# The order of the three products of a split matmul: the low activation before the low weight

## The chip, the core and the metric

The kernel runs on one core of one Trainium2 chip. The metric is the device time of one execution in microseconds (us), as the median of several runs. Beside the timed runs there is one profiled execution, with a trace of every instruction of each engine. In the rows PE is the matmul engine, PEld its weight load, DVE the vector engine, ACT the scalar engine, POOL the GpSimd engine and SP the queue that issues most transfers.

## The reference

One layer of a streaming encoder, 256 frames of 2048 channels in float32. A gated feed-forward block, a mixer with two branches, and a second feed-forward block follow each other, each added to the residual stream.

```python
h = rms_norm(x, ffn1_norm[l])
x = x + 0.5 * swiglu(h, ffn1_w_gate[l], ffn1_w_up[l], ffn1_w_down[l])      # 2048 -> 2 x 5504 -> 2048
h = rms_norm(x, mix_norm[l])
proj = h @ w_in[l]                                                          # 2048 -> 11280 columns
(gq, gk, gv, gz, ga, gb, aq, ak, av, gate_gdn, gate_att) = jnp.split(proj, split_at, axis=-1)
o_gdn = gdn_branch(...)                                                     # gated DeltaNet, 8 heads
o_att = chunk_attention_branch(...)                                         # banded softmax, 8 heads
merged = (jax.nn.sigmoid(gate_gdn) * (o_gdn @ w_branch_gdn[l])
          + jax.nn.sigmoid(gate_att) * (o_att @ w_branch_att[l]))
x = x + merged @ w_out[l]
h = rms_norm(x, ffn2_norm[l])
x = x + 0.5 * swiglu(h, ffn2_w_gate[l], ffn2_w_up[l], ffn2_w_down[l])
```

Nearly all arithmetic is in the dense products `h @ w`.

## The kernel before

**Split numbers.** The matmul engine is fed with a rounded 4-byte format (`F32R`). To keep the precision of float32, every operand is held as two tiles: a high part, which is the value rounded to that format, and a low part, which is what the rounding lost. A dense product is then three matmuls into the same PSUM bank: high activation by high weight, high activation by low weight, low activation by high weight. The function `product` (lines 527 to 535) issues these three, and it is the only place where dense products are issued. The activation block (128x128) is the operand that is loaded into the array, the weight piece (128 rows by up to 512 columns) is the one that streams.

**Where the parts come from.** Weights arrive from memory as `raw` tiles (two pieces of 512 KB each), issued by SP (L374, L376). ACT rounds them to the high part (`wh`, L422), DVE subtracts to get the low part (`wl`, L486). For about a third of the pieces the kernel uses a seven-product scheme in the manner of Strassen and Winograd: there DVE first builds sums of quarter blocks (`s`, L453 to L455), ACT rounds these (`sh`, L460) and the quarter blocks themselves (`w`, `v`, L458), and DVE subtracts once more (`sl`, and the low halves of `w` and `v`, L486). The activations are split in the same way (`xr`, `xf`, `hid`, L135/L136 and L191/L192), long before most of their uses.

**Stages.** A feed-forward block goes over 43 column tiles of the hidden layer in three chunks. Within a chunk, `seven` computes gate and up (banks `pf`) for four tiles at a time, the result is evacuated, gated, turned and split into `hid`; then `seven` computes the down product (banks `pd`) for two pairs of output groups. The name `pd_00` is chunk start 0, output groups 0 and 1; `pd_02` the groups 2 and 3; `pd_40` and `pd_42` are the same for the chunk that starts at 4. Partial sums of a chunk are added to memory tiles `xd` by accumulating transfers that POOL issues (L749, `xd<-ed`). Between the two feed-forward blocks stand the projections (`pav`, `paq`, `pak`, `pc`, `pz`, `pg`), the attention, the DeltaNet core, the merge and the output projection (`pwo`).

**What sets the order of the work.** The kernel is recorded through a tiling layer. It gives every tile a slot of a pool (most weight and activation tiles share one pool of 22 slots, `heap`), adds the semaphore waits, and it decides the order in which each engine's instructions stand: not simply the order of the Python lines, but by its own estimate of when operands are ready. Where it believes that a low part comes late, it moves products of another bank or of the next piece ahead. The kernel pins some orders by hand (`issue_after`). So a change of the written order of three lines also changes what stands beside them. Every engine then runs its own list strictly in that order, and SP and POOL their transfers.

**Line numbers in the profile.** Before, L533 is high by high, L534 high activation by low weight (it reads `wl`, `sl` or the low half of `w`, `v`), L535 low activation by high weight. In the changed kernel L534 is low activation by high weight and L535 is high activation by low weight.

Of the kernel before, what the change touches and what calls it, by code (L numbers as in the profile page):

```python
# [49 lines left out]
def block_kernel(ctx: ExitStack, tc: tile.TileContext, a: dict, out: bass.AP):  # L50
# [5 lines left out]
    nc = tc.nc  # L56
# [470 lines left out]
    def product(dst, act, wt, start, stop):  # L527

        (ah, al), (wh, wl) = act, wt
        dst = dst[:, : int(np.prod(wh.shape[1:]))]  # L530
        if len(wh.shape) == 3:
            dst = dst.rearrange("p (c x) -> p c x", x=P)
        nc.tensor.matmul(dst, ah, wh, start=start, stop=False)  # L533
        nc.tensor.matmul(dst, ah, wl, start=False, stop=False)  # L534
        return nc.tensor.matmul(dst, al, wh, start=False, stop=stop)  # L535

    def gemm(pss, kt, st, n):
        run(gemm_steps(pss, kt, st, n))
# [1 line left out]
    def gemm_steps(pss, kt, st, n):  # L540

        k = 0
        while k < kt:
            wh, wl, m = take_weights()
            assert m == n, (m, n)
            for w in zip(wh, wl):
                for t in range(2):
                    product(pss[t], st(k, t), w, k == 0, k == kt - 1)
                k += 1
            if k < kt:  # L550
                yield
# [8 lines left out]
    def seven(nm, n, fast, act, jobs=(), feed=None, pairs=range(KD // 2), out=None, base=None, kt=KD, late=None, acc=(1, 2, 3, 4)):  # L560
# [10 lines left out]
        def add(b, act, wt):  # L571
            if b not in banks:
                banks[b] = (acc_bank if b in (QUAD if late else acc) else core_bank)(f"p{nm}_{b}")[:, :n]
            done[b] += 1
            last = product(banks[b], act, wt, done[b] == 1, done[b] == size[b])
            if out and b in out and done[b] == size[b]:
                e = wide(f"e{nm}_{b}", n)
                nc.scalar.copy(e, banks[b])
                spare[b] = e
            return last  # L580
# [3 lines left out]
        for at_pair, j in enumerate(pairs):  # L584
# [6 lines left out]
            else:  # L591
                for s in range(2):
# [18 lines left out]
                    elif s == 0:  # L611
                        for k, w in kw:
                            for t in range(2):
                                add((2, 4)[t], act(j, 2 * k + t), w)
                        for b in (2, 4):
                            nc.vector.tensor_add(ev[b], banks[b], ev[b])
                        final[0](ev)
                    else:
                        for t, b in enumerate((3, 8)):
                            final[1 + t](ev)  # L620
                            if b == 8 and len(final) > 3:
                                cols = lambda w, x: [h[:, 2 * x : 2 * x + 2] for h in w]
                                for k, w in kw:
                                    product(banks[b][:, :T], act(j, 2 * k + t), cols(w, 0), False, k == 1)
                                nc.vector.tensor_add(ev[b], banks[b], ev[b])
                                final[3](0, 0, 4, ev)
                                rest = core_bank("rest")[:, :T]
                                for k, w in kw:
                                    product(rest, act(j, 2 * k + t), cols(w, 1), k == 0, k == 1)
                                final[3](1, 0, 2, ev)  # L630
                                nc.vector.tensor_add(ev[b][:, T:], rest, ev[b][:, T:])
                                final[3](1, 2, 2, ev)
                                continue
                            for k, w in kw:
                                add(b, act(j, 2 * k + t), w)
                            nc.vector.tensor_add(ev[b], banks[b], ev[b])
# [869 lines left out]
```

## Time and profile before

| | |
|---|---|
| median of 3 runs | 2083.09 us (2083.02 to 2084.07) |
| profiled execution, its own time | 2085.11 us |
| its span, first to last instruction | 2083.3 us |
| granted TensorE clock in it | 1.0 of full speed |
| PE busy | 2075.3 us, 9686 matmuls |
| DVE busy | 1891.8 us (91%) |
| ACT busy | 1227.7 us (59%) |
| matmuls of L533, L534, L535 | 2950 each |
| memory traffic | 437.74 MB, 210 GB/s over the span |

The profiled execution took 2.02 us more than the median of the runs; 1.8 us of its time lie outside the span. Matmuls overlap in the pipeline: one that is recorded as 0.39 us long is followed by the next one after about 0.23 us, so the distance between starts, not the recorded length, tells the engine's pace.

### The profile page before, as it was taken

What the parts mean: (1) busy time and instruction counts of PE and PEld (TensorE: products, weight loads), DVE (VectorE), ACT (ScalarE), POOL (GpSimd) and SP (SyncE); (2) the same over time, 40 slices, a digit from 0 to 9 for tenths busy, and PEclk for the clock granted to TensorE, in tenths of its full rate; (3) what the DMA queues carried; (4) which work ended last, traced back from release to release, by engine and by line L of the source; (5) the groups of instructions that cost most, each with busy time, mean ns of one, the idle gap of its engine ahead of it and who ended that gap; (6) DMA issues with size and microseconds to landing.
All of it is one profiled execution on the core that took longest, in us unless ns stands there. A gap on an engine that the chain in (4) does not pass through costs nothing.

```text
span 2083.3 us, 25887 instructions
## 1 busy us (share of the span) xinstructions
PE 2075.3 (100%) x9686; PEld 1734.0 (83%) x9686; DVE 1891.8 (91%) x2155; ACT 1227.7 (59%) x1282; POOL 78.7 (4%) x93
## 2 busy tenths in 40 slices
PE   9999999999999999999999999999999999999999
PEld 7888888887898988888888888888888888888897
DVE  7998999989998989987885798999998999899998
ACT  7664665645555756767645655556555555556554
POOL 0000110002001000000010000000000200011001
PEclk9999999999999999999999999999999999999999
DMA  9755986649858756744554466767665976569667
GB/s 331 236 184 167 264 261 210 201 146 268 258 187 229 267 181 198 229 156 142 187 163 151 142 220 215 241 201 224 209 195 163 283 241 198 176 188 311 193 187 202
DMA packets 402061, 437.74 MB, mean 210 GB/s; under 512 B 14976, under 2 KB 375056, under 8 KB 401680
## 3 DMA queue, kind: packets, MB, share of 16 engines
q1 hardware_dynamic: 390272, 415.04, 61.9%
q0 software_dynamic: 11520, 20.98, 5.8%
q8 instruction: 76, 1.25, 0.3%
q14 instruction: 49, 0.40, 0.1%
q10 hardware_dynamic: 144, 0.08, 0.0%
HBM read 407.72 MB, written 28.32 MB: 209 GB/s over the span
## 4 chain that ended last, share of the span: by engine, by line
PE 96%; DMA 2%; DVE 1%; ACT 0%; issue 0%; SPq 0%; ACTq 0%; DVEq 0%; POOLq 0%
PE pf L533 14%; PE pf L534 14%; PE pf L535 14%; PE pd L534 6%; PE pd L535 6%; PE pd L533 6%; PE pg L533 3%; PE pg L534 3%; PE pg L535 3%; PE pc L533 2%; PE pc L535 2%; PE pc L534 2%; PE pwo L533 1%; PE pwo L534 1%; PE pwo L535 1%; DMA xd<-ed 1%
## 5 line engine op out<-in xcount | busy, mean ns | idle before, releaser
L486 DVE TENSOR_TENSOR wl<-raw,wh 128x2048 fp32r<-128x2048 f32 (+5 forms) x252 | 546.0, 2171 | 49.7 <-ACT wh L422 12.9
L422 ACT CAST wh<-raw 128x2048 fp32r<-128x2048 f32 (+5 forms) x256 | 457.6, 1801 | 89.2 <-DVE wl L486 23.1
L460 ACT CAST sh<-s 128x2048 fp32r<-128x2048 f32 (+1 forms) x140 | 265.6, 1897 | 375.8 <-DVE s L455 351.6
L486 DVE TENSOR_TENSOR sl<-s,sh 128x2048 fp32r<-128x2048 f32 (+1 forms) x140 | 315.6, 2261 | 11.6 <-PE pd L534 3.3
L534 PE MATMUL pf<-wl,xr 128*128 128x512 f32 (+1 forms) x704 | 271.2, 385 | 0.1
L535 PE MATMUL pf<-wh,xr 128*128 128x512 f32 (+1 forms) x704 | 270.9, 385 | 0.0
L533 PE MATMUL pf<-wh,xr 128*128 128x512 f32 (+1 forms) x704 | 263.5, 387 | 0.1
L453 DVE TENSOR_TENSOR s<-raw 128x1024 f32<-128x1024 f32 (+1 forms) x140 | 168.7, 1205 | 17.7 <-PE pd L534 9.2
L458 ACT CAST w<-raw 128x1024 fp32r<-128x1024 f32 (+1 forms) x140 | 145.8, 1041 | 61.4 <-issue 11.8
L486 DVE TENSOR_TENSOR w<-raw,w 128x1024 fp32r<-128x1024 f32 (+1 forms) x140 | 168.8, 1206 | 9.4 <-ACT w L458 9.0
L534 PEld LDWEIGHTS pf<-wl,xr 128*128 128x128 f32 x704 | 132.4, 188 | 25.7 <-DVE wl L486 0.7
L533 PEld LDWEIGHTS pf<-wh,xr 128*128 128x128 f32 x704 | 132.2, 188 | 25.5 <-ACT xr L191 1.0
L535 PEld LDWEIGHTS pf<-wh,xr 128*128 128x128 f32 x704 | 132.3, 188 | 25.1 <-DVE xr L192 0.2
L534 PE MATMUL pd<-wl,hid 128*128 128x512 f32 x352 | 138.6, 394 | 0.0
L535 PE MATMUL pd<-wh,hid 128*128 128x512 f32 x352 | 137.4, 390 | 0.0
L749 POOL DMA_DIRECT2D xd<-ed x80 | 69.8, 964 | 1573.2 <-ACT ed L645 1246.3
L533 PE MATMUL pd<-wh,hid 128*128 128x512 f32 x352 | 128.5, 392 | 0.0
L458 ACT CAST v<-raw 128x512 fp32r<-128x512 f32 (+1 forms) x140 | 86.3, 617 | 71.0 <-PE pf L535 41.9
L534 PE MATMUL pf<-sl,xf 128*128 128x512 f32 (+1 forms) x288 | 110.8, 385 | 0.0
L535 PE MATMUL pf<-sh,xf 128*128 128x512 f32 (+1 forms) x288 | 110.4, 385 | 0.0
L533 PE MATMUL pf<-sh,xf 128*128 128x512 f32 (+1 forms) x288 | 108.8, 386 | 0.1
L486 DVE TENSOR_TENSOR v<-raw,v 128x512 fp32r<-128x512 f32 (+1 forms) x140 | 94.7, 676 | 3.2 <-ACT v L458 3.1
(564 smaller groups left out, 4403.7 us busy)
## 6 DMA issues: line engine op xcount, KB each, us to landing
raw<-wd SPq DMA_DIRECT2D x168, 512.0 KB, 5.1
raw<-wg SPq DMA_DIRECT2D x158, 512.0 KB, 4.6
raw<-wu SPq DMA_DIRECT2D x158, 512.0 KB, 5.7
raw<-wgt SPq DMA_DIRECT2D x64, 512.0 KB, 4.7
raw<-wa SPq DMA_DIRECT2D x48, 512.0 KB, 4.5
raw<-wc SPq DMA_DIRECT2D x48, 512.0 KB, 4.7
xd<-ed POOLq DMA_DIRECT2D x80, 256.0 KB, 7.1
raw<-wbr SPq DMA_DIRECT2D x32, 512.0 KB, 4.6
```

Source lines behind the costliest of these rows:

```text
L422: casts[i] = nc.scalar.copy(hi, src)
L453: nc.vector.tensor_sub(S[:, 0:2], R[:, 1], R[:, :, 0])
L458: nc.scalar.copy(hi, src)
L460: casts[i] = nc.scalar.copy(sh, s)
L486: last = subs[out[0][2]] = nc.vector.tensor_sub(lo, src, f32(hi))
L533: nc.tensor.matmul(dst, ah, wh, start=start, stop=False)
L534: nc.tensor.matmul(dst, ah, wl, start=False, stop=False)
L535: return nc.tensor.matmul(dst, al, wh, start=False, stop=stop)
L749: b: lambda e, dst=xd[d + dd][t]: nc.gpsimd.dma_start(dst, e, accum_op=ALU.add)
```

## The change

In `product` the second and the third matmul change places. The group still starts with high by high, and the one that closes the accumulation (`stop`) is now the one that reads the low weight. The operands, the number of matmuls, the tiles and the transfers are the same.

```diff
         nc.tensor.matmul(dst, ah, wh, start=start, stop=False)
-        nc.tensor.matmul(dst, ah, wl, start=False, stop=False)
-        return nc.tensor.matmul(dst, al, wh, start=False, stop=stop)
+        nc.tensor.matmul(dst, al, wh, start=False, stop=False)
+        return nc.tensor.matmul(dst, ah, wl, start=False, stop=stop)
```

The order in which the instructions stand changes on four engines; the list of SP is the same row by row. Three places matter for what follows.

The first is the matmul engine in the down product `pd_00`, where a new plain weight piece (`wh_1691`, `wl_1692`) begins and a seven-product piece (`w_1713`) follows it. Before:

```order
L533 MATMUL pd_00_2_1574<-wh_1691,hid_3_1573 128x512 [waits Activation_49]
L533 MATMUL pd_00_4_1578<-wh_1691,hid_3_1573 128x512
L533 MATMUL pd_00_3_1588<-wh_1691,hid_3_1573 128x512
L533 MATMUL pd_00_8_1592<-wh_1691,hid_3_1573 128x512
L533 MATMUL pd_00_1_1663<-w_1713,hid_2_1256 128x512 [waits Activation_49]
L534 MATMUL pd_00_1_1663<-w_1713,hid_2_1256 128x512 [waits DVE_49]
L534 MATMUL pd_00_2_1574<-wl_1692,hid_3_1573 128x512 [waits DVE_49]
```

The same place in the changed kernel:

```order
L533 MATMUL pd_00_2_1574<-wh_1691,hid_3_1573 128x512 [waits Activation_49]
L534 MATMUL pd_00_2_1574<-wh_1691,hid_3_1573 128x512
L533 MATMUL pd_00_4_1578<-wh_1691,hid_3_1573 128x512
L534 MATMUL pd_00_4_1578<-wh_1691,hid_3_1573 128x512
L533 MATMUL pd_00_3_1588<-wh_1691,hid_3_1573 128x512
L535 MATMUL pd_00_2_1574<-wl_1692,hid_3_1573 128x512 [waits DVE_49]
L535 MATMUL pd_00_4_1578<-wl_1692,hid_3_1573 128x512
```

The first product that reads the low weight stood behind six others of this piece and the next; now it stands behind five. The gap that was filled with high products of other banks is filled with low-activation products.

The second place is the matmul engine at the start of a gate and up piece `pf_16`, where a plain piece (`wh_2154`, `wl_2155`) is followed by a seven-product piece (`w_2180`, `sh_2187`). Before:

```order
L533 MATMUL pf_16_8_2282<-wh_2154,xr_1_132 128x512 [waits Activation_49]
L533 MATMUL pf_16_1_2215<-w_2180,xf_2_206 128x512
L534 MATMUL pf_16_1_2215<-w_2180,xf_2_206 128x512 [waits DVE_49]
L535 MATMUL pf_16_1_2215<-w_2180,xf_2_206 128x512
L533 MATMUL pf_16_6_2223<-sh_2187,xf_2_206 128x512 [waits Activation_49]
L533 MATMUL pf_16_7_2227<-sh_2187,xf_2_206 128x512
L534 MATMUL pf_16_2_2219<-wl_2155,xr_1_132 128x512 [waits DVE_49]
```

In the changed kernel:

```order
L533 MATMUL pf_16_8_2282<-wh_2154,xr_1_132 128x512 [waits Activation_49]
L534 MATMUL pf_16_8_2282<-wh_2154,xr_1_132 128x512
L533 MATMUL pf_16_1_2215<-w_2180,xf_2_206 128x512 [waits Activation_49]
L534 MATMUL pf_16_1_2215<-w_2180,xf_2_206 128x512
L535 MATMUL pf_16_2_2219<-wl_2155,xr_1_132 128x512 [waits DVE_49]
L535 MATMUL pf_16_4_2231<-wl_2155,xr_1_132 128x512
```

The two products of `sh_2187` have gone from here: they now stand behind all products of the plain piece, 30 matmuls after the piece's first one instead of 7. The same happens in `pd_02` and `pd_42` (before, the first product of `sh` stands behind 7 others and that of `wl` behind 8; now `wl` behind 6, and `sh` behind 30).

The third place is POOL's list at the end of the seven-product part of `pd_40`, where the accumulating transfers of this stage stand; the same move is in `pd_00`, in both feed-forward blocks.

```order
 L749 DMA xd_82<-ed_40_0_3766 128x512
+L749 DMA xd_82<-ed_40_2_3745 128x512
 L749 DMA xd_83<-ed_40_2_3768 128x512
-L749 DMA xd_82<-ed_40_2_3745 128x512
-L749 DMA xd_83<-ed_40_4_3756 128x512
 L749 DMA xd_85<-ed_40_3_3769 128x512
 L749 DMA xd_84<-ed_40_1_3767 128x512
+L749 DMA xd_83<-ed_40_4_3756 128x512
```

Two transfers into the same tile `xd_82` now stand directly behind each other, and the first one into `xd_83` stands behind both. On DVE and ACT some tens of neighbouring instructions change places, nearly all at the ends of the seven-product parts; no instruction is added or dropped on any engine.

## The prediction

> **What bounds the kernel now.** I read the page first: who is busy, the clock, the chain that ended last.
>
> ```profile
> span 2083.3 us, 25887 instructions
> PE 2075.3 (100%) x9686; PEld 1734.0 (83%) x9686; DVE 1891.8 (91%) x2155; ACT 1227.7 (59%) x1282; POOL 78.7 (4%) x93
> PEclk9999999999999999999999999999999999999999
> PE 96%; DMA 2%; DVE 1%; ACT 0%; issue 0%; SPq 0%; ACTq 0%; DVEq 0%; POOLq 0%
> ```
>
> The matmul engine never rests, at full clock, and 96% of the chain is its own work. But its recorded lengths overlap, so I asked the view by windows for each of the three lines over the whole span (columns: window, length, PE busy and count, PEld busy and count, clock, DMA share, GB/s), in the order L533, L534, L535.
>
> ```profile
> 0.00:2083.30 2083.30, 1106.34 (x2950) 553.80 (x2950) 1.00 0.68 210
> 0.00:2083.30 2083.30, 1136.89 (x2950) 554.40 (x2950) 1.00 0.68 210
> 0.00:2083.30 2083.30, 1133.50 (x2950) 554.10 (x2950) 1.00 0.68 210
> ```
>
> There are 2950 groups of three, and each of the 8850 products loads its own activation block: 554 us / 2950 = 188 ns on all three lines, although L533 and L534 of a group use the same block. The order of time shows how far apart the starts are in a quiet stretch, and in a short run of L533 alone.
>
> ```profile
> 24.17 0.39 PE L533 MATMUL pf<-wh,xf 128*128 128x512 f32 x1
> 24.40 0.39 PE L534 MATMUL pf<-wl,xf 128*128 128x512 f32 x1
> 24.62 0.39 PE L535 MATMUL pf<-wh,xf 128*128 128x512 f32 x1
> ...
> 28.25 0.39 PE L533 MATMUL pf<-wh,xf 128*128 128x512 f32 x1
> ```
>
> From 24.17 to 28.25 six groups start: 4.08 us / 18 = 0.227 us per product, and none of the three steps stands out. So the 188 ns of a load lie wholly under the product that runs.
>
> What is not pace is waiting. The views by source line list what the engine, loads included, sat idle for ahead of each product: first L533, then L534, then L535.
>
> ```profile
>   ACT sh L460: 6.8, 6
> ```
> ```profile
>   DVE wl L486: 5.8, 18
>   DVE sl L486: 1.3, 4
> ```
> ```profile
>   DVE xr L192: 0.6, 2
> ```
>
> That is some 14 us in 30 waits, of which a change in this order can move L534's: it waits for low weights 22 times, 7.1 us. L535, which takes its place, hardly waits: activations are early. What sets these waits is DVE, as four windows on the down products `pd_02` and `pd_42` show (columns: PE, PEld, DVE, ACT, POOL busy; clock, DMA share, GB/s).
>
> ```profile
> 240.00:250.00 10.00, 10.00 (x46) 8.26 (x45) 9.98 (x11) 4.53 (x5) 1.72 (x2) 1.00 1.10 319
> 490.00:500.00 10.00, 7.75 (x34) 6.12 (x34) 7.38 (x8) 4.60 (x5) 1.73 (x2) 1.00 1.10 294
> 1630.00:1640.00 10.00, 10.00 (x46) 8.27 (x45) 10.00 (x10) 6.30 (x5) 0.00 (x0) 1.00 1.10 319
> 1880.00:1890.00 10.00, 10.00 (x46) 8.26 (x45) 10.00 (x11) 5.05 (x4) 1.01 (x2) 1.00 1.10 324
> ```
>
> There DVE has no idle time at all (but for the second window, where it waits itself): for a few microseconds DVE, not the matmul engine, sets the pace, four times over.
>
> **The change part by part.** *Pace.* 8850 products before and after, with the same operands. New is only which neighbour follows which: after high by high comes a new activation block with the same weight. The trace has that pair where the planner put products of one weight piece in a row:
>
> ```profile
> 206.85 2.29 DVE L486 TENSOR_TENSOR wl<-raw,wh 128x2048 fp32r<-128x2048 f32 x1
> 207.68 1.07 PE L533 MATMUL pd<-wh,hid 128*128 128x512 f32 x4
> 208.59 0.39 PE L533 MATMUL pd<-w,hid 128*128 128x512 f32 x1
> 208.82 0.39 PE L534 MATMUL pd<-w,hid 128*128 128x512 f32 x1
> 209.19 0.19 PEld L534 LDWEIGHTS pd<-wl,hid 128*128 128x128 f32 x1 [0.41 <-DVE wl L486]
> 209.53 0.39 PE L535 MATMUL pd<-wh,hid 128*128 128x512 f32 x1
> ```
>
> Four products of L533 from 207.68 to 208.59: 0.91 / 4 = 0.227 us, as in the quiet stretch. Term: 0. The rounding of the rows leaves about 0.01 us over 4 steps, 2 ns a step; times 2950 that is 6 us either way, and since the six groups above average the same 0.227 I take 0.
>
> *A wait for a low weight that stays.* In the same rows DVE ends `wl` at 206.85 + 2.29 = 209.14, and the load follows at 209.19. PE would have gone on at 208.82 + 0.227 = 209.05, so it loses 0.14; then the next step takes 209.53 - 209.19 = 0.34 instead of 0.227, since a load that starts late is not hidden: 0.11 more. A wait costs 0.25 us here. "Low weight last" suggests that such waits go. They don't: the planner now puts five products ahead of that load where it put six. If DVE keeps its times, this wait grows by 0.23 us. Bounds for such a place: +0.23 (DVE unmoved) and -0.25 (gone).
>
> *A wait for the sums that goes.* At `pf_16` the chain is ACT's rounding `sh`:
>
> ```profile
> 268.77 1.92 ACT L460 CAST sh<-s 128x2048 fp32r<-128x2048 f32 x1 [1.91 <-DVE s L455]
> 270.31 0.39 PE L535 MATMUL pf<-w,xf 128*128 128x512 f32 x1
> 270.74 0.74 PE L533 MATMUL pf<-sh,xf 128*128 128x512 f32 x2
> 271.32 0.40 PE L534 MATMUL pf<-wl,xr 128*128 128x512 f32 x1
> ```
>
> The step into `sh` takes 0.43 us instead of 0.227, and from 270.74 to 271.32 two products take 0.58 instead of 0.45: 0.33 us lost. The view of L460 lists who waited for it; four loads of `pf` did:
>
> ```profile
>   PEld pf L533: 1.8, 4
> ```
>
> In the changed order these products stand 30 matmuls after the start of the piece instead of 7, 23 x 0.227 = 5.2 us later: these waits go, 4 x 0.33 = -1.3 us.
>
> *What stands ahead of them.* But the same stretch (198 to 271 us) has the waits for `wl` before it, which now come one or two products earlier (0.23 to 0.45 us). A delay that DVE sets is not added up, it is caught up: if DVE's times don't move, PE reaches the end of the stretch when DVE lets it, and what the last wait no longer costs an earlier one has cost already. Then the four stretches give 0. If DVE moves with PE, since it takes slots that PE's products free, the whole -1.3 is gained. I take -0.7.
>
> *The long wait.* The largest loss is at 496:
>
> ```profile
> 480.25 12.44 DMA raw<-wd
> 492.82 1.23 DVE s L453
> ```
> ```profile
> 496.38 0.39 PE L535 MATMUL pd<-w,hid 128*128 128x512 f32 x1
> 496.90 2.28 DVE L486 TENSOR_TENSOR wl<-raw,wh 128x2048 fp32r<-128x2048 f32 x1
> 499.02 0.50 PE L533 MATMUL pd<-sh,hs 128*128 128x512 f32 x1 [2.25 <-ACT sh L460]
> 499.36 0.39 PE L534 MATMUL pd<-wl,hid 128*128 128x512 f32 x1
> ```
>
> A weight transfer needed 12.44 us, against the page's usual time:
>
> ```profile
> raw<-wd SPq DMA_DIRECT2D x168, 512.0 KB, 5.1
> xd<-ed POOLq DMA_DIRECT2D x80, 256.0 KB, 7.1
> ```
>
> It ran beside the accumulating transfers `xd<-ed`. PE loses 499.02 - 496.38 - 0.227 = 2.4 us, and 0.11 after it. In the changed order `sh` is wanted 5.2 us later, but `wl` of the plain piece after six products instead of eight, and DVE ends it only at 496.90 + 2.28 = 499.18, nearly when `sh` came. So the wait changes its name (DVE `wl` for ACT `sh`) and stays: before, nine products had started by 499.36; now six by then, 3 x 0.227 = 0.68 later, less the 0.11 that one wait less costs and the 0.12 by which `wl` was ready early: +0.45 at that place, given back at the next two waits, which no longer bind. Term 0; bounds +0.45 and, if the transfer lands as usual, -2.5.
>
> *Small ones.* One more wait for `wl` goes in each block at the three-tile piece (0.2 us each, bounded by the 7.1 above: -0.3 together). At the very start and at the first projection `al` is wanted one product earlier: the two waits of L535, 0.6 us in all, may grow by 0.23 each; at the start the next wait, for `wl`, shrinks by as much. +0.2.
>
> Sum: 0 - 0.7 + 0 - 0.3 + 0.2 = -0.8 us. The profiled execution took 2085.11 us, 1.8 of it outside its span; it becomes 2084.3. The median of the runs stood 2.0 lower, so 2083.09 - 0.8, **2082.3 us**.
>
> **The rivals.**
>
> *Slower: the transfers collide more often (8%).* POOL's list now has two transfers into one `xd` tile in a row; the second must wait until the first has landed (7.1 us), and those behind it wait too and move towards the weight transfers of `pd_42`. For: DMA share 1.10 in all four windows, and one of the four has lost 2.4 us already; DVE is full in the other three, so a late landing there reaches PE. Against: POOL's last transfers of the group depend on the same landings as before. It decides where a landing takes more than about 12.44 - 2.5 = 10 us. All three others: 3 x 2.5 = +7.5, 2089.8 us.
>
> *Faster: the stalls dissolve (10%).* The transfer at 480 lands in time (-2.5), the four `sh` waits go whole (-1.3) and half of the 22 waits for low weights too (7.1 / 2 = -3.5): -7.3, less +0.2: 2076 us. For: low weights have the longest chain, and they are now read last in each group. Against: the order above, which does not use that; only where no product is moved up is 0.227 us won.
>
> *The shared block is lost (2%).* High by high and high by low were neighbours on the same activation block; the change parts them. If the array kept the block and the second load cost less than the first, the parting would cost up to a step's difference. The rows show 188 ns for each line and no longer step where the block changes; with the 2 ns that they leave open: +6 us, 2089 us. [...]
>
> *The change does less than it says.* Where the planner fills the gaps as before, the order of three lines is a renaming: 2083.1, inside the forecast.
>
> **How the numbers follow.** 0.2%, about what a measurement of this kernel can tell from no change, is 4.2 us. The forecast (80%) has its own range of 2080.6 to 2084.0: -2.2 to +0.9, the bounds of the stretches and the small waits. Faster by over 4.2 us needs the second rival (10%) and little else; slower the first, or the third (2%), or both in part: 9%. The same: 81%. To leave out no more than two in ten I go to 2078.8 and 2086.5, part of the way to either rival.
>
> **What would show it.** Right: three times 2950 products and loads of 188 ns; 0.227 us from start to start in a quiet stretch; the waits of L533 for `sh` down from six to one or two; L535 takes over the waits for `wl` and `sl`, 15 to 22 of them, 4 to 8 us; DVE full in the four windows. Wrong: a pace other than 0.227; a new idle time of over 1 us near 245, 1633 or 1884; landings of `raw<-wd` over 10 us at more than one place; or waits for low weights gone altogether.

## The result, and the profile after

| | median us | runs from … to |
|---|---|---|
| before | 2083.84 | 2082.43 … 2090.45 (22) |
| changed | 2081.35 | 2080.19 … 2083.41 (22) |

Ratio 0.9986, 95% interval 0.998 to 0.9992: 2.5 us between the medians. The spread shrank too, from 8 us to 3. (A few executions of the kernels below took far longer than all others of the same kernel, up to 4252 us, and the kernel before once took 8975; the ratios leave them out.) The profiled execution of the changed kernel took 2082.94 us, its span 2081.0, 2.3 us less than before.

The page of the changed kernel, its span and its chain (which could be followed back only to 258.8 us, so that its shares add up to 88%; the eleven instructions fewer than before are all of semaphores):

```profile
span 2081.0 us, 25876 instructions
PE 83%; DVE 2%; DMA 2%; ACT 1%; issue 0%; SPq 0%; ACTq 0%; DVEq 0%
```

The three lines over the whole span, L533, L534, L535 in that order (window, length, PE busy and count, load busy and count, clock, DMA share, GB/s):

```profile
0.00:2081.00 2081.00, 1142.79 (x2950) 554.10 (x2950) 1.00 0.68 210
0.00:2081.00 2081.00, 1135.90 (x2950) 554.19 (x2950) 1.00 0.68 210
0.00:2081.00 2081.00, 1120.75 (x2950) 552.39 (x2950) 1.00 0.68 210
```

The counts are the same, and a load still takes 188 ns (554.1 / 2950). The pace did not move (20 steps from 23.68 to 28.22 us in the changed kernel, 0.227 each); the waits did. By source line, what the engine sat idle for ahead of a product (us, times): L533, then L534, now the low activation, then L535, now the low weight.

```profile
  DVE eg L662: 1.6, 2
  ACT xr L191: 0.8, 1
```
```profile
  DVE xr L192: 1.5, 3
```
```profile
  DVE wl L486: 6.5, 13
  DVE sl L486: 2.5, 8
```

The waits for ACT's `sh` (6 entries, 6.8 us) are gone. The low weight's 22 entries (7.1 us) became 21 (9.0 us), fewer for `wl`, twice as many for `sl`. These lists need care. A long wait leaves the load and the product idle and is counted twice: the six entries for `sh` are five waits (the long one at 496 us stands there with 2.67 and with 2.25), and the 21 are 19. And idle time is not lost time. Measured by the starts of the products, as what goes beyond the usual step at the wait and at the step behind it, the waits for low weights cost 3.8 us before and 5.1 after, those for `sh` 3.7 before (2.5 of it the long one) and nothing after. The list of waits by pair (total, times, longest, all us) shows what is new:

```profile
PE pg L533 <- DVE eg L662: 0.6, 1, 0.6
PE pd L535 <- DVE wl L486: 0.6, 1, 0.6
PE pf L535 <- DVE wl L486: 0.4, 1, 0.4
```

The four windows, with the same columns as before (PE, PEld, DVE, ACT, POOL; clock, DMA share, GB/s):

```profile
240.00:250.00 10.00, 10.00 (x46) 8.29 (x45) 10.00 (x11) 4.90 (x4) 0.86 (x1) 1.00 1.10 299
490.00:500.00 10.00, 10.00 (x46) 8.28 (x45) 10.00 (x11) 4.77 (x5) 1.63 (x2) 1.00 1.10 300
1630.00:1640.00 10.00, 10.00 (x46) 8.29 (x45) 10.00 (x9) 6.72 (x6) 0.00 (x0) 1.00 1.09 332
1880.00:1890.00 10.00, 10.00 (x46) 8.29 (x45) 10.00 (x8) 7.16 (x6) 0.00 (x0) 1.00 1.09 319
```

DVE is full in all four, now at 490 too. The window at 490, which had 34 products, has 46 like the others: the long wait at 496 is gone. The rows around it say how. First the order of time before (POOL's and SP's issues: start, length, count), then after, then the changed kernel's DMA issues in the stretch from 479.35 to 480.9 us (count, KB each, median us to landing).

```profile
476.08 0.86 POOL L749 DMA_DIRECT2D xd<-ed  x1 [204.36 <-ACT ed L645]
478.38 0.86 POOL L749 DMA_DIRECT2D xd<-ed  x1 [1.44 <-DVE ed L647]
...
479.84 1.09 SPq L374 DMA_DIRECT2D raw<-wd  x2
```
```profile
476.11 0.86 POOL L749 DMA_DIRECT2D xd<-ed  x1 [203.80 <-ACT ed L645]
480.48 3.53 POOL L749 DMA_DIRECT2D xd<-ed  x4 [3.51 <-DMA xd<-ed]
...
479.00 0.92 SPq L374 DMA_DIRECT2D raw<-wd  x2
```
```profile
raw<-wd SPq DMA_DIRECT2D x2, 512.0 KB, 4.4
```

Before, two accumulating transfers had been issued when SP asked for the two halves of the weight piece from 479.84 on, a third came at 480.44, and the second half landed after 12.44 us. After, POOL's list has the second transfer to the same `xd` tile next; it waits until the first has landed and starts at 480.48, behind the weight requests, which land in 4.4 us.

### The profile page after: what moved, and what is told of

Its sections match the earlier page's. It is cut to its first block, busy times and chain, and to the rows that moved or that the text cites. A ratio compares the mean times of both kernels' runs of the same rounds, so it can differ in the third digit from the quotient of the medians.

```text
span 2081.0 us, 25876 instructions
## 1 busy us (share of the span) xinstructions
PE 2073.4 (100%) x9686; PEld 1734.1 (83%) x9686; DVE 1892.3 (91%) x2155; ACT 1228.1 (59%) x1282; POOL 78.9 (4%) x93
## 4 chain that ended last, share of the span: by engine, by line
PE 83%; DVE 2%; DMA 2%; ACT 1%; issue 0%; SPq 0%; ACTq 0%; DVEq 0%
PE pf L535 11%; PE pf L534 11%; PE pf L533 11%; PE pd L535 5%; PE pd L534 5%; PE pd L533 5%; PE pc L533 2%; PE pc L534 2%; PE pc L535 2%; PE pg L533 2%; PE pg L534 2%; PE pg L535 2%; PE pwo L533 1%; PE pwo L535 1%; PE pwo L534 1%; PE hid L145 1%
## 5 line engine op out<-in xcount | busy, mean ns | idle before, releaser
L533 PE MATMUL pf<-wh,xr 128*128 128x512 f32 (+1 forms) x704 | 271.8, 386 | 0.0
L534 PE MATMUL pf<-wh,xr 128*128 128x512 f32 (+1 forms) x704 | 270.5, 384 | 0.1
L535 PE MATMUL pf<-wl,xr 128*128 128x512 f32 (+1 forms) x704 | 265.5, 385 | 0.4 <-DVE wl L486 0.4
L535 PEld LDWEIGHTS pf<-wl,xr 128*128 128x128 f32 x704 | 132.1, 188 | 26.1 <-DVE wl L486 1.3
L533 PEld LDWEIGHTS pf<-wh,xr 128*128 128x128 f32 x704 | 132.3, 188 | 25.2 <-ACT xr L191 0.8
L534 PEld LDWEIGHTS pf<-wh,xr 128*128 128x128 f32 x704 | 132.1, 188 | 25.0 <-DVE xr L192 0.4
L533 PE MATMUL pd<-wh,hid 128*128 128x512 f32 x352 | 137.9, 392 | 0.0
L534 PE MATMUL pd<-wh,hid 128*128 128x512 f32 x352 | 136.9, 389 | 0.0
L535 PE MATMUL pd<-wl,hid 128*128 128x512 f32 x352 | 133.4, 393 | 0.6 <-DVE wl L486 0.6
L534 PE MATMUL pf<-sh,xf 128*128 128x512 f32 (+1 forms) x288 | 110.7, 384 | 0.0
L533 PE MATMUL pf<-sh,xf 128*128 128x512 f32 (+1 forms) x288 | 110.1, 384 | 0.0
L535 PE MATMUL pf<-sl,xf 128*128 128x512 f32 (+1 forms) x288 | 109.9, 384 | 0.0
```

Of the source, the lines that this page charges most:

```text
L534: nc.tensor.matmul(dst, al, wh, start=False, stop=False)
L535: return nc.tensor.matmul(dst, ah, wl, start=False, stop=stop)
```

## The experiments

Two theories to begin with. **T**: the gain is this place, POOL's order kept the weight transfer free. **Q**: it is the order of the products, the regular waits for `sh` and the low weights. The kernels were timed in three batches, each with its own runs of the kernel before, and each kernel is set against those: 2083.87 us for the first four, 2083.04 for the next four, 2082.96 for the last.

**POOL's order alone, put in and taken out.** The product order stays; the eight transfers of `pd_00` and `pd_40` are issued in a list written out by hand (the second kernel: the changed product order, with the list of before).

```diff
+        if out and nm.endswith(("_00", "_40")):
+            seq = ((0, 2), (1, 2), (0, 4), (0, 8), (0, 3), (1, 4), (1, 8), (1, 3))
+            at = None
+            for kind, b in seq:
+                with ExitStack() as order:
+                    if at:
+                        order.enter_context(tc.issue_after(at.ins))
+                    at = out[b]((ev, spare)[kind][b])
+            return None
```

> The product order of before, H W A, with every list of PE, DVE, ACT and SP as before; only POOL's list of the eight accumulating transfers of pd_00 and pd_40 (four places) is put into the order it has in the changed kernel (xd_82, xd_82, xd_83, ... in place of xd_82, xd_83, xd_82, ...). Theory T (transfers): the 2.4 us wait near 496 goes because the weight transfer queued at 480 lands in about 5 us in place of 12.4; no other wait moves: 2.0 to 2.5 us faster than before, so about 2081.5 us, most of what the change won. Rival Q (the order of products): POOL's order does nothing by itself, the landing stays near 12 us or the wait is replaced: within 0.5 us of before, 2083.8 us.

> The changed product order, H A W, with every list of PE, DVE, ACT and SP as in the changed kernel; only POOL's list of the eight accumulating transfers of pd_00 and pd_40 goes back to the order of before. Theory T: the long landing near 480 us comes back (over 10 us), and the first product that reads a low weight of that piece waits over 2 us near 496: about 2083.8 us, 2.5 us slower than the changed kernel. Rival Q: it keeps 2081.4 us, since products, not transfers, made the gain.

Measured: the new POOL order in the kernel before 2084.76 us (ratio 1.0002, interval 0.9993 to 1.001), the old one in the changed kernel 2082.91 us (0.9993, 0.9984 to 1.0001). The second lies between what T and Q had given for it (2083.8 and 2081.4) and decides nothing by itself; with the first, T falls. Its mechanism works: with the new POOL order the same two transfers land in 4.5 us and there is no wait at 496.

```profile
raw<-wd SPq DMA_DIRECT2D x2, 512.0 KB, 4.5
```

But no time is won; the low weights of L534 are now waited for longer, 8.6 us where it was 5.8:

```profile
  DVE wl L486: 8.6, 23
```

The added waits are short ones in `pf`, and three of them, at 532, 1666 and 1918 us, end chains that begin with weight transfers of 14.8 to 15.2 us: the late landings have moved. And the old POOL order with the new products has no late landing either:

```profile
480.01 1.75 POOL L758 DMA_DIRECT2D xd<-ed  x2 [2.82 <-DVE ed L647]
```
```profile
raw<-wd SPq DMA_DIRECT2D x2, 512.0 KB, 4.4
```

There DVE's `ed` came later, so the second transfer again started behind the request (479.18). So a landing at 480 is decided by a microsecond in either list, and one execution's long wait there does not set the median. Before's own profiled execution took 2085.11 us, 2.0 above the median of its first three runs and 1.3 above that of the 22; the wait (2.4) may account for it, but the profiled execution of the changed kernel stands 1.6 above its median too, and no wait in it costs over 0.9.

**Where in the program.** The new order in the down products only, and everywhere but there.

```diff
-    def product(dst, act, wt, start, stop):
+    def product(dst, act, wt, start, stop, swap=False):
...
-        nc.tensor.matmul(dst, ah, wl, start=False, stop=False)
-        return nc.tensor.matmul(dst, al, wh, start=False, stop=stop)
+        second, third = ((al, wh), (ah, wl)) if swap else ((ah, wl), (al, wh))
+        nc.tensor.matmul(dst, *second, start=False, stop=False)
+        return nc.tensor.matmul(dst, *third, start=False, stop=stop)
...
-            last = product(banks[b], act, wt, done[b] == 1, done[b] == size[b])
+            last = product(banks[b], act, wt, done[b] == 1, done[b] == size[b], nm[0] == "d")
```

> H A W in the down products (names beginning pd) alone, H W A in all others; the lists of DVE and ACT change in 28 rows each and POOL's takes the order of the changed kernel. Theory T: the 2.5 us wait near 496 goes, one or two new waits of pd for wl come (0.84 us near 260, 0.16 us four times), the four waits of pf for sh (0.33 us each) stay: -1.0 to -2.0 us, 2082.3 us. Rival Q (what counts is that waits for sums and low weights dissolve in all products): the gain goes by the number of products, down 1/3 of it: -0.8 us, 2083.0 us.

> H A W in all products but the down ones, which keep H W A; POOL's list stays as before. Theory T: the 2.5 us wait near 496 stays, the four waits of pf for sh (0.33 us each) and one near 613 (0.38) go, new waits of some 0.7 us near 530 and 0.7 us near 1224 come: 0 to -1.0 us, 2083.3 us. Rival Q: two thirds of the gain or more, -1.6 us or better, 2082.0 us.

Measured: down products only 2081.62 us (0.9989, 0.9981 to 0.9998), 2.25 us faster, the whole gain and more than either theory gave it (2082.3 and 2083.0); all but the down products 2098.02 us (1.0058, 1.0041 to 1.0076), **14 us slower** by the medians and 12 by the ratio, nine runs from 2085.2 to 2103.8. (That one has `!=` and `swap=True`.) Both halves together are the changed kernel, so they don't add up. Neither theory expected the second. Its waits by pair, and two pieces of its chain of waits (start, us):

```profile
PE pf L533 <- ACT sh L460: 11.4, 3, 4.7
PE pd L533 <- ACT sh L460: 2.8, 1, 2.8
```
```profile
1623.61 12.95 DMA raw<-wd
...
1908.98 15.29 DMA raw<-wu
```

Four waits for sums, at 271, 526, 1639 and 1921 us; all four stand behind weight transfers, of 12.8, 15.1, 13.0 and 15.3 us. And each costs more than it lasts. The windows around the first (columns as above, the clock is the third number from the right):

```profile
271.00:274.00 3.00, 0.86 (x4) 0.38 (x2) 0.16 (x1) 2.42 (x3) 1.23 (x2) 1.00 1.08 323
...
276.00:278.00 2.00, 2.00 (x7) 1.51 (x6) 2.00 (x3) 0.75 (x1) 0.00 (x0) 0.50 1.11 232
```

After this wait of 2.4 us the granted clock fell to 0.50 for about 3 us, and products started 0.42 us apart:

```profile
276.29 0.63 PE L533 MATMUL pf<-wh,xr 128*128 128x512 f32 x1
276.71 0.63 PE L535 MATMUL pf<-wh,xr 128*128 128x512 f32 x1
```

By the starts of the products this place lost 4.1 us in all. This is the rival that I had called "the transfers collide more often", in a kernel that makes half of the change.

**Theory C: what the transfers cost.** If late weight transfers beside the accumulating ones make these waits, smaller accumulating transfers must end them. Three kernels have 16 of 128 rows in each (112 rows of these sums are left out); their lists of PE, DVE, ACT and SP are those of the kernel they come from, and POOL's has as many transfers in the same order.

```diff
-                    b: lambda e, dst=xd[d + dd][t]: nc.gpsimd.dma_start(dst, e, accum_op=ALU.add)
+                    b: lambda e, dst=xd[d + dd][t]: nc.gpsimd.dma_start(dst[:16], e[:16], accum_op=ALU.add)
```

> The kernel before with 16 of the 128 rows in each accumulating transfer xd<-ed (the other 112 rows of these sums are left out of the result); number and order of all instructions as before. Theory C (the weight transfers that run beside these transfers land late, and the product that then waits for the rounded sums loses 2 to 5 us in some executions): the landing near 480 us takes about 5 us in place of 12.4, the wait near 496 is gone, the spread of the runs (2081.7 to 2087 in the kernel before) shrinks to under 2 us and the time falls to the lowest runs of before, 2081.7 us. Rival P (the product order does it, transfers nothing): within 0.5 us of before, 2083.8 us.

> The changed kernel with 16 of the 128 rows in each accumulating transfer xd<-ed (112 rows of these sums left out of the result). Theory C: it has hardly any collision left to lose: 0 to -1 us, 2080.4 to 2081.4 us; its gain over the kernel before with the same cut falls from 2.4 us to the four waits for sums and the small ones, 0.5 to 1.3 us. Rival P: the gain over the kernel before with the same cut stays 2.4 us.

> The kernel with H A W in all products but the down ones (2098.0 us), with 16 of the 128 rows in each accumulating transfer xd<-ed (112 rows of these sums left out of the result). Theory C (its four long waits for sh at 271, 526, 1639 and 1921 us come from weight transfers that land after 12 to 15 us beside the accumulating transfers): those waits and the half clock behind them go, about 2081.8 us as the kernel before with the same cut, spread under 2 us. Rival O (its mixed order itself leaves the products too early for the sums, whatever the transfers do): 2090 us or more, the waits for sh stay over 2 us.

| | full transfers | 16 rows |
|---|---|---|
| H W A (before) | 2083.04 | 2081.80 (11 runs: 2081.5 to 2082.4) |
| H A W (changed) | 2081.35, against 2083.84 | 2080.03 (10 of 11 runs: 2079.7 to 2081.0) |
| H A W but in the down products | 2098.02, against 2083.87 | 2082.91, against 2082.96 |

C holds: the 14 us of the mixed order are gone, and before's runs lie within 0.9 us of each other. The landings show it directly: the longest of any weight transfer was 14.5 us in the kernel before, 15.0 in the changed one and 15.3 in the mixed order; with 16 rows it is 9.9, 10.3 and 10.2. The weight transfers at 480 us landed in 4.4 us behind one accumulating transfer and in 12.44 behind two with a third at their heels; how the DMA engines divide their time between the two kinds no run here shows.

With the transfers out of the way the two orders stand 1.77 us apart, 2081.80 and 2080.03, in one batch. C had given 0.5 to 1.3 for this, P 2.4; it lies between. That is the **regular** part of the gain, and the lists of waits show it. The kernel before with 16 rows, L533 then L534:

```profile
  ACT sh L460: 1.8, 4
```
```profile
  DVE wl L486: 5.8, 18
  DVE sl L486: 1.3, 4
```

The changed kernel with 16 rows, L535 (L533 has no `sh`):

```profile
  DVE wl L486: 3.3, 8
  DVE sl L486: 2.5, 8
```

26 waits with 8.9 us of idle time became 16 with 5.8, and by the starts of the products 5.0 us became 3.4, nearly the whole 1.77. (Idle time counts from the end of the load before; a quiet product has 0.04 of it, 0.227 - 0.188.) The four waits for `sh` had cost 0.30 us each, 1.2 in all, and one for `wl` at 611 us 0.38; four for `wl` near 229 us and its like (0.11 each) gave way to four for `sl` (0.16), and four near 260 had cost next to nothing.

Where does this part come from? The new order in the down products alone, with full transfers, has the very list of low-weight waits that the changed kernel has with 16 rows (8 and 8, 3.3 and 2.5 us). The waits for `sh` stand in `pf`, but they follow the order of the down products, not that of `pf`: the list of L533 with the new order in the down products only, then in all but these and with 16 rows:

```profile
  ACT sh L460: 0.9, 4
```
```profile
  ACT sh L460: 2.0, 4
```

By the starts these cost 0.08 us each in the first and 0.35 in the second, where before they cost 0.30. With 16 rows the mixed order (2082.91) is also 1.1 us slower than the old one (2081.80, another batch). So the regular gain hangs on the down products; how their order shortens the waits for `sh` behind them was not taken apart further.

By this test late transfers cost the kernel before 1.2 us (2083.04 - 2081.80 in one batch) and the changed one 1.3 (2081.35 - 2080.03, from two batches). So most of the gain is regular. The 0.7 us between 1.77 and the 2.5 of the first result are less than the median of the kernel before moves from batch to batch (2082.96 to 2083.87), and go to neither theory; what the transfers did change is the tail of the runs (2090 before, 2083 after).

**The place of the low weight, and the neighbours.** A W H keeps the low weight in the middle and A H W keeps it last; both only exchange H and A, and their lists are those of before and of the changed kernel but for these names. W H A has it first.

```diff
A W H:  matmul(dst, al, wh, start)   matmul(dst, ah, wl)         matmul(dst, ah, wh, stop)
A H W:  matmul(dst, al, wh, start)   matmul(dst, ah, wh)         matmul(dst, ah, wl, stop)
W H A:  matmul(dst, ah, wl, start)   matmul(dst, ah, wh)         matmul(dst, al, wh, stop)
```

> The three products in the order A W H (low activation by high weight, high by low, high by high): the low weight stays in the middle, only H and A change places against the kernel before; every engine's list is that of before but for these names. Theory (pace does not depend on neighbours, the place of the low weight sets the waits): the kernel before again, 2083.8 us within 0.7, pitch 0.227 us. Rival S (what counts is which operands neighbouring products share): here W and H share the activation block as H and W did, so it would not move either; Rival A (the low activation's place matters): al is wanted first in each group, waits at the first projections grow by 0.23 to 0.45 us each, 2084.5 us.

> The order A H W: the low weight stays last as in the changed kernel, only H and A change places; every engine's list is that of the changed kernel but for these names. H and W are neighbours on one activation block again, which they are not in the changed kernel. Theory (the place of the low weight sets the waits, neighbours nothing): the changed kernel again, 2081.4 us within 0.7. Rival S (a shared block is worth something): faster than the changed kernel, by 2 ns a group or more: 6 us, 2075 us.

> The order W H A: the low weight first in each group. Theory (the place of the low weight among the three sets what the regular waits cost; last against middle gave 1.8 us without the collisions): the waits for wl and sl grow by about one product, 0.23 us, at each of 16 to 22 places, 3.5 to 5 us slower than before: 2087 to 2089 us. Rival F (the planner only fills what is free, the order of three lines is a renaming): 2083.5 us within 1.

Measured: A W H 2084.23 us (1.0004, 0.9995 to 1.0013), as before; A H W 2081.86 (0.9994, 0.9985 to 1.0003), within 0.5 us of the changed kernel although H and W share their activation block again; its interval doesn't tell it from before. In its profiled execution the first products stand 0.43 us apart up to 10 us, which costs about 2 us against the changed kernel. So neighbours are worth nothing that can be measured, and Rival S is out. Rival A is not: in both orders that begin with the low activation the first dense product starts at 5.8 us, in those that begin with high by high at 5.1 to 5.4, and 2084.23 fits it (2084.5) as well as the theory. The low weight's waits follow its place; A W H (L534), then A H W (L535):

```profile
  DVE wl L486: 6.9, 21
```
```profile
  DVE wl L486: 3.3, 8
```

W H A: 2101.26 us (1.0081, 1.0064 to 1.0098), 18 us slower, where I expected 3.5 to 5. Its L533 sits idle (36 waits, many counted twice, which cost 23 us by the starts of the products)

```profile
  DVE wl L486: 39.4, 45
  DVE sl L486: 4.0, 10
```

and in the order of time at the place that the prediction quoted for `pd`:

```profile
208.32 0.39 PE L535 MATMUL pd<-w,hid 128*128 128x512 f32 x1
209.48 0.50 PE L533 MATMUL pd<-wl,hid 128*128 128x512 f32 x1 [0.77 <-DVE wl L486]
```

A bank's products run in the order in which they are written: behind the one at 209.48 stand L534 at 209.81 and L535 at 210.05. With W first no product of the piece can start before its low weight; with W second each of the piece's four banks has one product that can, with W last two. That would be why the first step is worth much (18 us) and the second little (1.8): with W second 0.25 us or less was left of nearly every wait, and with W last the planner does not use all it could; at this place five products of the piece stand ahead in the changed kernel, where eight could.

**The upper bound.** High by low is computed with the high weight in place of the low one; DVE still makes every low weight.

```diff
-        nc.tensor.matmul(dst, ah, wl, start=False, stop=False)
+        nc.tensor.matmul(dst, ah, wh, start=False, stop=False)
```

> The kernel before with the high weight read in place of the low one in L534 (the high-by-low products are computed with wrong operands; DVE still computes every low weight): no product waits for a low weight any more, an upper bound for what its place can win. Theory: the waits for sums and the transfers then bind: 2079 to 2081 us, hardly better than the low weight last without collisions (2080.0). Rival: all 7.1 us of the waits for low weights come back, 2076.5 us.

Measured 2075.51 us (0.9962, 0.9947 to 0.9977), 7.5 us under before: the rival's number, but not by its reason. The 7.1 us are idle time, and by the starts of the products these waits cost only 3.8. In this run the waits for `sh` are gone as well, which had cost 1.2 us without the long one, and with them perhaps the 1.2 of the late transfers; a rest of about 1.3 us is not accounted for. There is no second limit close behind, and the change takes a quarter to a third of what is there.

**A version that was to beat both.** Half as many accumulating transfers: POOL, busy 4% of the span, first adds the two tiles of a block. The lists of PE, DVE, ACT and SP are those of the changed kernel.

```diff
-                put(ev[b])
-                put(spare[b])
+                nc.gpsimd.tensor_add(ev[b], spare[b], ev[b])
+                put(ev[b])
```

> The changed kernel; the two accumulating transfers of each block of a down product become one, after POOL has added the two tiles in SBUF: 40 transfers in place of 80 with the same sums; the lists of PE, DVE, ACT and SP are those of the changed kernel. Theory C (what the changed kernel still loses to late weight transfers is 1.3 us, 2081.4 against 2080.0 with the rows cut): about half of it or more comes back, 2080.0 to 2080.8 us. Rival V (POOL's additions take SBUF time from DVE, which is full in these stretches): 2081.5 to 2084 us, DVE's operations beside them longer than before.

Measured 2141.05 us (1.0274, 1.0258 to 1.0289): 58 us slower. Rival V, at many times the price. POOL's additions and DVE's operations beside them:

```profile
225.17 3.26 POOL L656 TENSOR_TENSOR ed<-ed,ed 128x512 f32<-128x512 f32 x1 [224.72 <-DVE ed L646]
...
229.73 5.82 POOL L656 TENSOR_TENSOR ed<-ed,ed 128x512 f32<-128x512 f32 x3
```
```profile
227.80 1.18 DVE L486 TENSOR_TENSOR v<-raw,v 128x512 fp32r<-128x512 f32 x1
...
230.10 2.08 DVE L453 TENSOR_TENSOR s<-raw 128x1024 f32<-128x1024 f32 x1
232.10 2.31 DVE L486 TENSOR_TENSOR w<-raw,w 128x1024 fp32r<-128x1024 f32 x1
...
269.22 3.30 DVE L486 TENSOR_TENSOR v<-raw,v 128x512 fp32r<-128x512 f32 x1
```

The first takes 1.18 us where it takes 0.68 elsewhere, the next two 2.08 and 2.31 for 1.22, and the last 3.30 for 0.68. Over the whole span DVE is busy 1941.5 us in place of 1892.3, 49 us more for the same operations. These four read two SBUF inputs, but a `wl` at 225.00, beside the first addition and also with two, keeps its 2.28 us; whether it is SBUF time that the two engines share no run here shows. The granted clock falls too, to 0.989 over the span and to 0.50 from 1651 to 1657 us, and PE waits for what DVE is late with, up to 5.5 us at a time:

```profile
PE pf L535 <- DVE wl L486: 21.9, 4, 5.5
PE pd L535 <- DVE sl L486: 11.6, 4, 3.0
```

No kernel here that adds up all its sums beats the changed one; the down products alone (2081.62) equal it.

## Why the prediction was right, point by point

It said 2082.3 us in 2078.8 to 2086.5, most likely no difference over 0.2%. The time is 2081.35, the gain 0.14%, within 0.2%. The direction was right, the size was a third (0.8 of 2.5 us). That the time lies inside says little for the terms, since the range holds no change as well. That the sum came within 1 us is partly luck: the term for the waits for sums was too small, and the long wait stood in it as a fixed loss. (The forecast's own range should begin at 2080.9, 2.2 under 2083.09, not at 2080.6.)

- **Pace, 0.** Right: 2950 loads of 188 ns on each line, and the neighbours tested by themselves in A H W and A W H.
- **The wait for a low weight that stays.** Right: eight places in `pd`, 0.26 us each in both traces. DVE moved with PE (the `wl` quoted at 206.85 starts at 206.20 in the changed kernel), so the bound of +0.23 was not touched.
- **The waits for sums at `pf_16` and `pf_32`, taken at -0.7 of -1.3.** All four are gone in the changed kernel; by the starts of the products they had cost 1.2 us. The step that failed is "What stands ahead of them": that a delay which DVE sets is only caught up. DVE is as full as the prediction said, 45.9 of the 46 us ahead of 271 before and 45.5 in the changed kernel with 16 rows. But in the changed order the end of the stretch no longer hangs on it: with 16 rows ACT ends `sh` at 270.30 and PE first uses it at 275.59. The new `sl` waits gave back only 4 x 0.05 us. The term should have been nearly whole, -1.0. Its reason, the later place of these products, is half of the story at best: with the new order in the down products alone they stay where they were and still lose only 0.08 us each.
- **Small ones, -0.3 and +0.2.** About right: 0.38 at one of the places of the first, and at the first projection the wait for the low activation cost 0.70 us in place of 0.40 (profiled executions).
- **The long wait, term 0, "the wait changes its name".** Wrong for the profiled execution: the wait did not come back as a wait for `wl`, because the transfer landed in time; the bound of -2.5 came true. The step overlooked that the change also moves when POOL starts its transfers. But its place in the sum was wrong before that. A landing which a microsecond decides is not a fixed term; with small transfers the wait is absent in both orders, and 1.77 us of the gain stay. So the 2.5 us of the profiled place and the 2.5 us between the medians are alike by chance, as far as the runs show.
- **From the profile to the median.** The sum started from an execution 2.0 us above the median and subtracted the 2.0 again. That the surplus was about as large as the one long wait was there to be seen, and a reason to give that wait no fixed term.
- **What would show it.** The low-weight entries came to 21 and 9.0 us, where 15 to 22 and 4 to 8 was said; `sh` to none, one or two was said. One sign of being wrong did appear, landings of `raw<-wd` over 10 us at more than one place: 12 transfers. But it was no sign, for the kernel before has 10 of them. None of the 12 cost over 0.9 us: a late landing costs something only where its piece is wanted at once.
- **Waits taken from the lists.** "Some 14 us in 30 waits" counts the long one twice, and the 7.1 us for low weights, from which the second rival took half, had cost 3.8.
- **The rivals.** The slower one, collisions, did not happen in the change but in half of it (+14 us), at a price that the prediction had too low: it priced a late landing at 2.5 us, and with the clock behind it one cost 4.1 to 6.6. "The stalls dissolve" had the `sh` waits right and far too much for the low weights, which cost less in all after the change only with small transfers (3.8 to 3.4). The shared block was worth nothing.

Not settled: why late transfers cost the mixed order so much in nearly every run, and the kernel before seldom. What sets the moments of its requests was not tried.

## What to carry to other kernels

Where several products go into one bank, put last the one whose operand has the longest chain: what seems to count is how many products of the piece can run without that operand (0, 4 or 8 here: +18, 0, -1.8 us). Before a long wait goes into a sum, set the profiled execution beside the median of the runs; a wait that a single late transfer makes belongs into the range. Take the cost of a wait from the starts of the products, not from a list of idle times. An idle engine isn't a free one: beside POOL's additions single operations of DVE took up to 4.8 times as long.

## What the runs showed of the hardware that I had not expected

**The clock falls after short waits, but not always.** The wait of 2.4 us at 271 in the mixed order was followed by a granted clock of 0.50; one of the same length at 496 in the kernel before was not:

```profile
499.00:502.00 3.00, 2.98 (x13) 2.48 (x14) 3.00 (x5) 1.45 (x2) 0.00 (x0) 1.00 1.08 341
```

The version with POOL's additions has the same wait for `sl`, 3.0 to 3.1 us, four times, once in each of the four places. Behind the first (at 236) and the third (at 1648):

```profile
239.00:242.00 3.00, 2.92 (x13) 2.41 (x14) 3.00 (x3) 2.39 (x2) 0.00 (x0) 1.00 1.11 171
...
1651.00:1654.00 3.00, 2.75 (x7) 2.17 (x8) 2.39 (x2) 1.78 (x1) 0.00 (x0) 0.50 1.12 196
```

Where the clock fell in the mixed order, each of the four waits lost 1.6 to 1.8 us more than it lasted. The length of the wait alone does not decide it: 2.4 us were enough at 271 in the mixed order, 2.4 at 496 in the kernel before and 3.0 at 236 with POOL's additions were not. What does decide it no run here shows.

**Two engines, one load.** POOL's 40 additions took 2.2 us on average and DVE was busy 49 us longer, 1.2 us for each, about the length of the shortest addition (1.28 us). Most operations of 512 or 1024 columns that read two SBUF tiles took 1.6 to 4.8 times as long beside them (those quoted above 1.7 to 4.8); `ed<-pd,ed`, with one input in PSUM, kept its 0.68 us, and `wl` and `sl` of 2048 columns kept theirs (the whole groups on average 2.18 and 2.28 us, 2.18 and 2.27 in the changed kernel).
